# Sums of the lower weights in DRAM at fixed places of each upper block, one quarter to a block and two in the tenth

## The chip, the cores and the metric

The kernel runs on one core of one Trainium2 chip. The metric is the device time of one execution in microseconds (us). Before the change it is 2028.64 us, the median of three runs (2025.68 to 2032.72).

## What is computed

One layer of a streaming encoder on 512 tokens of width 2048, in fp32: a modulated RMS norm, a combined projection into a recurrent and an attention group, an output projection, and then a SwiGLU feed-forward layer of hidden width 5632. Only the last part and its modulation matter here:

```python
mod = c_act @ w_ada[l] + b_ada[l]
sh1, sc1, gt1, sh2, sc2, gt2 = jnp.split(mod, 6, axis=-1)
...
h2 = modulate(rms_norm(x, g_ffn[l]), sh2, sc2)
gate, up = jnp.split(h2 @ w_up[l], 2, axis=-1)
x = x + gt2[:, None, :] * ((jax.nn.silu(gate) * up) @ w_down[l])
```

## The kernel before

Every matrix is split into a high and a low part (`wsplit`: ScalarE rounds the high part in a line at 271, VectorE subtracts it in the line behind, both 128x1024), and each product is three matmuls of 128x512.

The **upper** stage (`h2 @ w_up`) has a short beginning in the ordinary way and then ten blocks, `b` = 0 to 9, of seven products each (`ORDER`: 4, 5, 1, 7, 6, 2, 3), the seven of a Strassen scheme instead of eight. A block needs four units of weights, each two tiles of 128x2048 (`uw`), loaded by SyncE in the order A, C, B, D. In the numbered names `uw3_20` is block 3, unit 2 (0 is A, 1 C, 2 B, 3 D), half 0. VectorE adds one unit into another between products (`sum_unit`). A product has eight steps `j`, each of twelve matmuls for the two steps of one weight split; a half of a product is four steps, so a block has 14 halves. The results of a block are turned in the next one (`back`) and written to DRAM by SyncE (`td`, eight writes a block).

In the upper blocks VectorE also works off the modulation `gt2` in pieces (class `Gt2`): SyncE loads a broadcast row of `c_d` and rows of `adaT` into six pages from step (3, 3) of a block, and VectorE reduces a piece at fixed steps from (4, 1) on.

The **lower** stage (`@ w_down`) follows in four phases. It too is a scheme of seven products over four blocks of `w_down` for each of eleven groups of 512 rows; such a group is called a quarter here, `q` = 0 to 10. Two of its operands, `s2d[q]` and `s4d[q]`, are sums of weights that lie in DRAM. `sums24(q, n)` makes them in four steps: step 0 lets SyncE copy `wdn[0]` into `s2d` and `wdn[1]` into `s4d`, DRAM to DRAM, in halves of 512 KB; steps 1 and 2 let GpSimd add `wdn[2]` and `wdn[3]` into `s2d` with accumulating DMAs; step 3 adds `s2d` into `s4d`. They are first read in phases 2 and 3.

```python
elif n < 3:
    dram_sum(s2d[q], wdn[n + 1, q])
else:
    dram_sum(s4d[q], s2d[q])
```

A scheduler orders each engine's instructions by the order of the code and by priorities (`tc.high_priority`: weight loads, splits and unit sums run `AHEAD` of their place; `tc.issue_after` places an instruction behind another in its queue). Each queue then runs in order: an instruction that waits holds all behind it. The steps of the sums run at the code's own place, and nothing but the data before them holds them at run time.

Before the change a counter over all halves sets the places: from half 2 on, every third half makes the next step, so a quarter takes 12 halves while a block has 14, and a quarter's places wander through the blocks.

Of the kernel before, what the change touches and what calls it, by code (L numbers as in the profile page):

```python
# [60 lines left out]
KEEP = (2, 8, 2)  # L61
GT2_STEPS = ((4, 1), (4, 2), (4, 3), (4, 5), (4, 7), (5, 5), (6, 1))
GT2_N = (6, 6, 6, 6, 6, 6, 7, 7, 7, 7)
SUMS_AT, SUMS_PER = 2, 12
BU_PART = (0, 5, 10, 16)
BUP_STEP = 3
NQ = FT // 4
# [7 lines left out]
def block_kernel(ctx, tc, xT, crow, adaT, vecs, bfr, w1, wyr, wqkv0, wqkv, wgate, wout, wup0, wups, wdn, outT):  # L75
# [17 lines left out]
    def page(name, tag, shape=None):  # L93
        return pgp.tile(shape or [P, S], F32, tag=tag, name=name, bufs=TAGS[tag])
# [180 lines left out]
    def mm(ps, l, r, start, stop):  # L275
        nc.tensor.matmul(ps, lhsT=R(l), rhs=R(r), start=start, stop=stop)  # L276
# [228 lines left out]
    def add(hooks, n, *fns):  # L505
        hooks.setdefault(n, []).extend(fns)
        return hooks
# [587 lines left out]
    def dram_sum(out, src):  # L1095
        for i in range(2):
            cs = slice(i * 1024, (i + 1) * 1024)
            nc.gpsimd.dma_start(out=out[:, cs], in_=src[:, cs], accum_op=ALU.add)  # L1098

    def sums24(q, n):  # L1100
        if n == 0:
            with tc.issue_after((up_loads or stream_loads)[-1]):
                for i in range(2):
                    cs = slice(i * 1024, (i + 1) * 1024)
                    nc.sync.dma_start(out=s2d[q][:, cs], in_=wdn[0, q, :, cs])
                    nc.sync.dma_start(out=s4d[q][:, cs], in_=wdn[1, q, :, cs])
# [4 lines that stand above are left out]
# [36 lines left out]
    NBLK = (FT - 2 * STD) // 4  # L1147
# [24 lines left out]
    def prod_weights(p, b, un):  # L1172
        with tc.high_priority(offset=AHEAD):
            if p == 4:
                un[U_A] = load_unit(b, U_A)
                un[U_C] = load_unit(b, U_C)
            elif p == 5:
                sum_unit(un[U_A], un[U_C])
            elif p == 1:
                un[U_B] = load_unit(b, U_B)  # L1180
            elif p == 7:
                sum_unit(un[U_C], un[U_B])
            elif p == 6:
                sum_unit(un[U_A], un[U_B])
            elif p == 2:
                un[U_D] = load_unit(b, U_D)
            else:
                sum_unit(un[U_A], un[U_D])
            src = un[{4: U_A, 5: U_A, 1: U_B, 7: U_C, 6: U_A, 2: U_D, 3: U_A}[p]]
        for q in range(4):  # L1190
            with tc.high_priority(offset=AHEAD):
                hi, lo = wsplit(src[q // 2][:, (q % 2) * 1024:(q % 2 + 1) * 1024], 1024, f"up{b}_{p}_{q}")
            for i in range(2):
                yield 2 * q + i, hi[:, i * S:(i + 1) * S], lo[:, i * S:(i + 1) * S]

    def back(g, b, f, last=False):
        pt = misc(f"up_t{b}_{f}") if last and f else rgp(f"up_t{b}_{f}")
        for t in range(NT):
            nc.tensor.transpose(out=pt[:, t * P:(t + 1) * P], in_=g[t][:, f * P:(f + 1) * P], identity=ident)
        o = page(f"uo{b}_{f}", "d")  # L1200
        with tc.high_priority(offset=EVAC):
            nc.scalar.activation(o, pt, AF.Copy)
        keep_act(o, 2 * STD + 4 * b + f, last)

    gt2_left = [(r, i) for r in range(4) for i in range(KT)]
    hk = {}
    nprod = halves = 0
    for b in range(NBLK):
        un, keep_ = {}, {}
        gt2 = Gt2(gt2_left[:GT2_N[b]])  # L1210
        del gt2_left[:GT2_N[b]]
        add(hk, (3, 3), gt2.loads)
        for _, at in zip(range(GT2_N[b]), GT2_STEPS):
            add(hk, at, gt2.piece)
        for i, p in enumerate(ORDER):
            pool = misc if (nprod + 2) % 3 == 2 else acc
            nprod += 1
            ps = [pool(f"up{b}_{p}p{t}") for t in range(2)]
            for j, hi, lo in prod_weights(p, b, un):
                th, tl = T[p][j]  # L1220
                for t in range(2):
                    c_ = slice(t * P, (t + 1) * P)
                    mm(ps[t], th[:, c_], hi, j == 0, False)
                    mm(ps[t], th[:, c_], lo, False, False)
                    mm(ps[t], tl[:, c_], hi, False, j == 7)
                for fn in hk.get((i, j), ()):
                    fn()
                if j % 4 == 3:
                    n = halves - SUMS_AT
                    halves += 1  # L1230
                    if 0 <= n < SUMS_PER * NQ and n % SUMS_PER % 3 == 0 and n % SUMS_PER < 12:
                        sums24(n // SUMS_PER, n % SUMS_PER // 3)
            if b + i == 0:
                up_last()
            if p in (4, 5, 1, 7):
                keep_[p] = []
                for t in range(2):
                    w = page(f"us{b}_{p}{t}", "c") if p != 7 else ap_.tile([P, S], F32, tag="x", name=f"us{b}_{p}{t}", bufs=2)
                    with tc.high_priority(offset=EVAC):
                        nc.scalar.activation(w, ps[t], AF.Copy)  # L1240
                    keep_[p].append(w)
            elif p == 6:
                u2 = [page(f"uu{b}_{t}", "c") for t in range(2)]
                s4, s5, s1, s7 = (keep_[k] for k in (4, 5, 1, 7))
                with tc.high_priority(offset=EVAC):
                    for t in range(2):
                        nc.vector.tensor_add(u2[t], ps[t], s1[t])
                with tc.high_priority(offset=POST):
                    for t in range(2):
                        nc.vector.tensor_sub(s7[t], u2[t], s7[t])  # L1250
                        nc.vector.tensor_sub(u2[t], u2[t], s5[t])
                        nc.vector.tensor_sub(s4[t], s4[t], s7[t])
                        nc.vector.tensor_sub(s5[t], s5[t], s7[t])
            else:
                g, u = (s1, s4) if p == 2 else (u2, s5)
                with tc.high_priority(offset=EVAC):
                    for t in range(2):
                        nc.vector.tensor_add(g[t], ps[t], g[t])
                with tc.high_priority(offset=EVAC):
                    for t in range(2):  # L1260
                        nc.scalar.activation(g[t], g[t], AF.Silu)
                        nc.vector.tensor_mul(g[t], g[t], u[t])
        hk = {(1, 1 + 2 * f): [lambda g=s1 + u2, b=b, f=f: back(g, b, f)] for f in range(4)}
# [231 lines left out]
```

## Time and profile before

| | |
|---|---|
| median of three runs | 2028.64 us |
| the profiled execution's own time | 2028.19 us |
| its span, from first to last instruction | 2026.5 us |
| its granted TensorE clock | 0.999 |
| TensorE busy | 2005.5 us (99%), 9330 matmuls |
| VectorE busy | 1678.2 us (83%) |
| ScalarE busy | 986.8 us (49%) |
| GpSimd busy | 109.8 us (5%) |
| DMA queue q1 (SyncE's and ScalarE's issues) | 454.99 MB, 65.4% of 16 engines' span |
| DMA queue q0 (GpSimd's issues) | 39.59 MB, 11.2% |

Rows of the profile name an engine (PE is TensorE, PEld its weight load, DVE VectorE, ACT ScalarE, POOL GpSimd, SP SyncE, with a q for issuing), a line, an operation and output<-input, with buffer numbers left out (`gt` is `gt2_0_12`, `uw` any weight tile). A row of the timeline begins with its start and duration in us and ends with the idle time before it and what ended that. DMA rows give count, KB each and the median us from issue to landing.

### The profile page before, as it was taken

Reading aid. Unit: us, or ns where it says so; the run is one execution under the profiler, and the core shown is the slowest. Engines: PE = TensorE matmul, PEld = TensorE weight load, DVE = VectorE, ACT = ScalarE, POOL = GpSimd, SP = SyncE. Lnnn points to the kernel's source line nnn. Section 1 sums busy time; section 2 is a strip of 40 time slices with the busy share of each in tenths; the row PEclk is TensorE's granted clock in tenths of the full one; section 3 lists DMA queues with packets and bytes.
Section 4 is the critical chain, followed back from the end, with each engine's and each line's share of the span. In section 5 each row is a group of like instructions: output and inputs, shape, how many; then the busy total and the mean of one; then the engine's idle time right before and its main releaser. Section 6 shows DMA issues by size and latency. Waiting matters only on the chain.

```text
span 2026.5 us, 25606 instructions
## 1 busy us (share of the span) xinstructions
PE 2005.5 (99%) x9330; PEld 1688.7 (83%) x9330; DVE 1678.2 (83%) x2300; ACT 986.8 (49%) x1362; POOL 109.8 (5%) x138
## 2 busy tenths in 40 slices
PE   9999999999999999999999999999999999999999
PEld 7889988898888888888887888888888888888887
DVE  8999788877787769898797888988988977777786
ACT  4433446775422257544544544445445455445443
POOL 0000100111000000000010000000000100000000
PEclk9999999999999999999999999999999999999999
DMA  9989866557679874779698868878696677778793
GB/s 354 346 296 336 281 213 209 199 170 258 225 256 319 327 259 143 184 201 270 187 280 236 207 235 228 208 261 238 187 289 186 222 249 245 253 239 295 257 331 119
DMA packets 173683, 496.33 MB, mean 245 GB/s; under 512 B 18434, under 2 KB 41138, under 8 KB 169459
## 3 DMA queue, kind: packets, MB, share of 16 engines
q1 hardware_dynamic: 162372, 454.99, 65.4%
q0 software_dynamic: 11040, 39.59, 11.2%
q8 instruction: 73, 1.20, 0.2%
q14 instruction: 54, 0.44, 0.1%
q10 hardware_dynamic: 144, 0.11, 0.0%
HBM read 458.93 MB, written 93.36 MB: 273 GB/s over the span
## 4 chain that ended last, share of the span: by engine, by line
PE 87%; DVE 6%; issue 4%; DMA 2%; ACT 1%; POOL 0%; DVEq 0%; POOLq 0%; ACTq 0%
PE up_2p L276 5%; PE up_6p L276 5%; PE up_3p L276 5%; PE up_5p L276 5%; PE up_1p L276 5%; PE up_7p L276 5%; PE up_4p L276 5%; PE w1p L276 4%; PE dn4p L276 3%; PE dn6p L276 3%; PE dn3p L276 3%; PE dn1p L276 3%; PE dn2p L276 3%; PE dn7p L276 3%; PE dn5p L276 3%
## 5 line engine op out<-in xcount | busy, mean ns | idle before, releaser
L1170 DVE TENSOR_TENSOR uw<-uw,uw 128x2048 f32<-128x2048 f32 x80 | 182.5, 2282 | 2.0 <-DMA uw<-in_wups 2.0
L178 DVE SCALAR_TENSOR_TENSOR ada<-ada,c_b 128x1024 f32<-128x1024 f32 x96 | 116.7, 1221 | 46.3 <-DMA ada<-in_adaT 46.1
L271 ACT ACTIVATE up_1h<-uw 128x1024 fp32r<-128x1024 f32 x70 | 74.4, 1063 | 118.9 <-PE up_6p L276 21.6
L271 ACT ACTIVATE up_0h<-uw 128x1024 fp32r<-128x1024 f32 x70 | 74.3, 1062 | 115.0 <-PE up_4p L276 16.6
L272 DVE TENSOR_TENSOR up_1l<-uw,up_1h 128x1024 fp32r<-128x1024 f32 x70 | 85.3, 1219 | 36.1 <-ACT up_1h L271 36.1
L272 DVE TENSOR_TENSOR up_0l<-uw,up_0h 128x1024 fp32r<-128x1024 f32 x70 | 85.4, 1220 | 33.6 <-ACT up_0h L271 33.5
L271 ACT ACTIVATE up_3h<-uw 128x1024 fp32r<-128x1024 f32 x70 | 74.4, 1063 | 71.7 <-PE up_2p L276 14.9
L271 ACT ACTIVATE up_2h<-uw 128x1024 fp32r<-128x1024 f32 x70 | 74.2, 1060 | 58.4 <-PE up_2p L276 16.5
L272 DVE TENSOR_TENSOR up_2l<-uw,up_2h 128x1024 fp32r<-128x1024 f32 x70 | 85.3, 1218 | 20.0 <-ACT up_2h L271 19.9
L272 DVE TENSOR_TENSOR up_3l<-uw,up_3h 128x1024 fp32r<-128x1024 f32 x70 | 85.2, 1217 | 10.3 <-ACT up_3h L271 10.3
L1098 POOL DMA_DIRECT2D s2d<-in_wdn x44 | 36.5, 842 | 624.2 <-DMA s2d<-in_wdn 624.2
L276 PE MATMUL w1p<-hph,w1l 128*128 128x512 f32 x128 | 49.8, 389 | 0.0
L276 PE MATMUL w1p<-hpl,w1h 128*128 128x512 f32 x128 | 49.8, 389 | 0.0
L222 DVE SCALAR_TENSOR_TENSOR gt<-gt,gt_None 128x512 f32<-128x512 f32 x64 | 43.0, 683 | 5.5 <-DMA gt<-in_adaT 5.5
L276 PE MATMUL w1p<-hph,w1h 128*128 128x512 f32 x128 | 42.6, 392 | 0.0
L188 DVE SCALAR_TENSOR_TENSOR ada<-ada,c_b 128x1024 f32<-128x1024 f32 x32 | 39.0, 1218 | 4.0 <-DMA ada<-in_adaT 4.0
L188 DVE SCALAR_TENSOR_TENSOR adf<-adf,c_b 128x1024 f32<-128x1024 f32 x32 | 39.0, 1219 | 0.3 <-DMA adf<-in_adaT 0.3
L631 ACT ACTIVATE bt<-bt,nm 128x128 f32<-128x128 f32 (+3 forms) x32 | 17.9, 561 | 34.8 <-DVE nm L629 34.5
L712 DVE SCALAR_TENSOR_TENSOR ba<-bw,sh,ba 128x512 f32<-128x512 f32 x45 | 32.2, 743 | 0.0
L616 POOL TENSOR_SCALAR_AFFINE_SELECT bt<-bt 128x128 f32<-128x128 f32 x32 | 22.8, 735 | 116.2 <-ACT bt L615 116.2
L437 ACT ACTIVATE hph<-x,A 128x512 fp32r<-128x512 f32 x16 | 11.6, 723 | 35.0 <-DVE A L434 35.0
L276 PEld LDWEIGHTS w1p<-hph,w1h 128*128 128x128 f32 x128 | 24.0, 188 | 5.4 <-issue 0.6
(2293 smaller groups left out, 6637.8 us busy)
## 6 DMA issues: line engine op xcount, KB each, us to landing
uw<-in_wups SPq DMA_DIRECT2D x160, 512.0 KB, 7.2
ada<-in_adaT SPq DMA_DIRECT2D x128, 512.0 KB, 5.4
s2d<-in_wdn POOLq DMA_DIRECT2D x44, 512.0 KB, 8.8
adf<-in_adaT SPq DMA_DIRECT2D x32, 512.0 KB, 6.0
gt<-in_adaT SPq DMA_DIRECT2D x64, 256.0 KB, 6.1
s2d<-in_wdn SPq DMA_DIRECT2D x22, 512.0 KB, 8.9
s4d<-in_wdn SPq DMA_DIRECT2D x22, 512.0 KB, 9.9
s4d<-s2d POOLq DMA_DIRECT2D x22, 512.0 KB, 8.2
```

What stands on the lines that cost most here:

```text
L178: nc.vector.scalar_tensor_tensor(out=t, in0=t, scalar=1.0, in1=cs, op0=ALU.mult, op1=ALU.mult, accum_out=ac)
L188: nc.vector.scalar_tensor_tensor(out=t, in0=t, scalar=1.0, in1=c_b[:, cs], op0=ALU.mult, op1=ALU.mult, accum_out=ada_acc[j][:, hf, i:i + 1])
L222: nc.vector.scalar_tensor_tensor(out=t, in0=t, scalar=1.0, in1=c, op0=ALU.mult, op1=ALU.mult, accum_out=gt2_acc[:, r, i:i + 1])
L271: tail_hi.append(nc.scalar.activation(R(hi[:, :n]), raw_ap, AF.Copy).ins)
L272: tail_lo.append(nc.vector.tensor_sub(R(lo[:, :n]), raw_ap, hi[:, :n]).ins)
L276: nc.tensor.matmul(ps, lhsT=R(l), rhs=R(r), start=start, stop=stop)
L437: nc.scalar.activation(R(h), xt, AF.Copy, scale=a)
L616: nc.gpsimd.affine_select(out=bt[:, b * P:n], in_=bt[:, b * P:n], pattern=[[-1, P]], compare_op=ALU.is_ge, fill=NEG, base=0, channel_multi ...
L631: nc.scalar.activation(p[:, :n], p[:, :n], AF.Exp, scale=-1.0, bias=nm, accum_out=sm)
L712: nc.vector.scalar_tensor_tensor(out=ba[j], in0=src, scalar=s1, in1=ba[j], op0=ALU.mult, op1=ALU.add)
L1098: nc.gpsimd.dma_start(out=out[:, cs], in_=src[:, cs], accum_op=ALU.add)
L1170: nc.vector.tensor_add(d_, d_, s_)
```

## The change

The counter goes. In blocks 0 to 8 the four steps of quarter `b` are made behind halves 1, 3, 9 and 12 of the block; in block 9 those of quarters 9 and 10 behind halves 0, 2, 4, 6 and 7, 9, 11, 13.

```diff
-SUMS_AT, SUMS_PER = 2, 12
+SUMS_STEPS = {1: 0, 3: 1, 9: 2, 12: 3}
+SUMS_LAST = {0: (9, 0), 2: (9, 1), 4: (9, 2), 6: (9, 3), 7: (10, 0), 9: (10, 1), 11: (10, 2), 13: (10, 3)}
...
-    nprod = halves = 0
+    nprod = 0
...
                 if j % 4 == 3:
-                    n = halves - SUMS_AT
-                    halves += 1
-                    if 0 <= n < SUMS_PER * NQ and n % SUMS_PER % 3 == 0 and n % SUMS_PER < 12:
-                        sums24(n // SUMS_PER, n % SUMS_PER // 3)
+                    n = 2 * i + j // 4
+                    if b < NBLK - 1 and n in SUMS_STEPS:
+                        sums24(b, SUMS_STEPS[n])
+                    elif b == NBLK - 1 and n in SUMS_LAST:
+                        sums24(*SUMS_LAST[n])
```

Weights are loaded ahead, so the rows around block 3's C and B units on SyncE's queue (`uw3_1` and `uw3_2`) run during block 2. Before, with `s2d3` and `s4d3` of quarter 3 and `s2d4`, `s4d4` of quarter 4, up to the first `td` write of block 3:

```order
L1105 DMA s2d3_6899<-in_wdn 128x1024
L1106 DMA s4d3_6910<-in_wdn 128x1024
L1105 DMA s2d3_6899<-in_wdn 128x1024
L1106 DMA s4d3_6910<-in_wdn 128x1024
L1163 DMA uw3_10_9505<-in_wups 128x1024 x2
L1163 DMA uw3_11_9508<-in_wups 128x1024 x2
L1163 DMA uw3_20_9702<-in_wups 128x1024 x2
L1163 DMA uw3_21_9705<-in_wups 128x1024 x2
L1105 DMA s2d4_6900<-in_wdn 128x1024
L1106 DMA s4d4_6911<-in_wdn 128x1024
L1105 DMA s2d4_6900<-in_wdn 128x1024
L1106 DMA s4d4_6911<-in_wdn 128x1024
```

The same place after the change:

```order
L1164 DMA uw3_10_9499<-in_wups 128x1024 x2
L1164 DMA uw3_11_9502<-in_wups 128x1024 x2
L1106 DMA s2d3_6899<-in_wdn 128x1024
L1107 DMA s4d3_6910<-in_wdn 128x1024
L1164 DMA uw3_20_9700<-in_wups 128x1024 x2
L1106 DMA s2d3_6899<-in_wdn 128x1024
L1164 DMA uw3_21_9703<-in_wups 128x1024 x2
L1107 DMA s4d3_6910<-in_wdn 128x1024
```

Quarter 4's four copies left this place for the one block later, and quarter 3's moved from ahead of C to around B. Before, quarter 8's copies stood on SyncE's queue between block 7's units in this same way:

```order
L1163 DMA uw7_10_11958<-in_wups 128x1024 x2
L1163 DMA uw7_11_11961<-in_wups 128x1024 x2
L1105 DMA s2d8_6904<-in_wdn 128x1024
L1106 DMA s4d8_6915<-in_wdn 128x1024
L1163 DMA uw7_20_12159<-in_wups 128x1024 x2
L1105 DMA s2d8_6904<-in_wdn 128x1024
L1163 DMA uw7_21_12162<-in_wups 128x1024 x2
L1106 DMA s4d8_6915<-in_wdn 128x1024
```

These rows of before are what the change makes of every block from 2 to 9. The tenth block has more. Around its C and B units on SyncE's queue, which run during block 8, stood, before, quarter 10's copies alone, ahead of C; after the change the rows from C on are:

```order
L1164 DMA uw9_10_13178<-in_wups 128x1024 x2
L1164 DMA uw9_11_13181<-in_wups 128x1024 x2
L1106 DMA s2d9_6905<-in_wdn 128x1024
L1107 DMA s4d9_6916<-in_wdn 128x1024
L1164 DMA uw9_20_13379<-in_wups 128x1024 x2
L1106 DMA s2d9_6905<-in_wdn 128x1024
L1164 DMA uw9_21_13382<-in_wups 128x1024 x2
L1107 DMA s4d9_6916<-in_wdn 128x1024
L1106 DMA s2d10_6906<-in_wdn 128x1024
L1107 DMA s4d10_6917<-in_wdn 128x1024
L1106 DMA s2d10_6906<-in_wdn 128x1024
L1107 DMA s4d10_6917<-in_wdn 128x1024
```

Eight copies stand there instead of four. On GpSimd's queue the end of the sums was, before, with the first late `td` write behind it:

```order
L1098 DMA s2d9_6905<-in_wdn 128x1024 x4
L1098 DMA s4d9_6916<-s2d9_6905 128x1024 x2
L1098 DMA s2d10_6906<-in_wdn 128x1024 x4
L1098 DMA s4d10_6917<-s2d10_6906 128x1024 x2
L1088 DMA td3_10_6895<-uo9_1_13860 256x1x256
```

After the change the same twelve sums stand there, with two of quarter 9's and one of quarter 10's exchanged:

```order
L1099 DMA s2d9_6905<-in_wdn 128x1024 x3
L1099 DMA s4d9_6916<-s2d9_6905 128x1024
L1099 DMA s2d9_6905<-in_wdn 128x1024
L1099 DMA s2d10_6906<-in_wdn 128x1024
L1099 DMA s4d9_6916<-s2d9_6905 128x1024
L1099 DMA s2d10_6906<-in_wdn 128x1024 x3
L1099 DMA s4d10_6917<-s2d10_6906 128x1024 x2
L1089 DMA td3_10_6895<-uo9_1_13860 256x1x256
```

Before, quarter 9's copies stood a block earlier than quarter 10's; now both stand in front of the tenth block, and so do their sums.

## Prediction

> **What bounds the kernel now.** I read the page first, then TensorE's waits, then the busy time of each upper block, then the queues around the one block that stands out. Blocks are counted from 0, as `b` in the code; "the tenth" is block 9. Times "in a block" run from its first matmul.
>
> ```profile
> span 2026.5 us, 25606 instructions
> PE 2005.5 (99%) x9330; PEld 1688.7 (83%) x9330; DVE 1678.2 (83%) x2300; ACT 986.8 (49%) x1362; POOL 109.8 (5%) x138
> ...
> PE up_6p L276 <- DVE up_2l L272: 3.6, 1, 3.6
> PE up_6p L276 <- DVE up_1l L272: 1.3, 1, 1.3
> ```
>
> TensorE is busy for 99% of the span. The two last rows are its waits between 800 and 1600 us, where all ten upper blocks lie: two waits, both in product 6, both on a VectorE split. The next rows give stretches cut at the first matmuls of blocks 2, 3, 4, 6, 7 and 9 (span, then busy time and count of PE, PEld, DVE, ACT and POOL, granted clock, DMA share, GB/s), and last the 4 us of the longer wait.
>
> ```profile
> 968.00:1046.40 78.40, 78.31 (x353) 64.58 (x352) 67.97 (x77) 38.23 (x44) 4.10 (x5) 1.00 0.75 225
> 1046.40:1131.70 85.30, 80.42 (x354) 65.57 (x353) 67.73 (x75) 38.19 (x44) 6.57 (x8) 0.98 0.86 236
> 1131.70:1209.80 78.10, 78.10 (x353) 64.56 (x352) 67.43 (x75) 38.21 (x44) 4.94 (x6) 1.00 0.80 217
> ...
> 1366.10:1444.20 78.10, 78.10 (x353) 64.56 (x352) 68.12 (x78) 38.21 (x44) 8.22 (x10) 1.00 0.93 256
> 1522.40:1600.60 78.20, 78.20 (x354) 64.61 (x353) 68.83 (x79) 39.26 (x46) 0.81 (x1) 1.00 0.63 202
> 1102.00:1106.00 4.00, 3.06 (x10) 2.45 (x11) 4.00 (x7) 0.00 (x0) 0.00 (x0) 0.79 0.78 311
> ```
>
> A block takes 78.1 to 78.2 us with TensorE busy throughout. Block 3 takes 85.3: 7.1 too many, of which 85.30 - 80.42 = 4.9 are waiting and 2.2 slower matmuls, at a granted clock of 0.79 behind the longer wait. Block 2 has 0.2 too many. So all that the upper stage can give back is 7.3 us, 0.36% of the time.
>
> Where block 3 loses it: VectorE's rows there, then the same ones in block 9.
>
> ```profile
> 1087.75 1.23 DVE L272 TENSOR_TENSOR up_0l<-uw,up_0h 128x1024 fp32r<-128x1024 f32 x1 [1.49 <-ACT up_0h L271]
> 1094.43 0.69 DVE L222 SCALAR_TENSOR_TENSOR gt<-gt,gt_None 128x512 f32<-128x512 f32 x1 [5.46 <-DMA gt<-in_adaT]
> ...
> 1099.46 2.29 DVE L1170 TENSOR_TENSOR uw<-uw,uw 128x2048 f32<-128x2048 f32 x1 [1.96 <-DMA uw<-in_wups]
> 1101.67 1.22 DVE L272 TENSOR_TENSOR up_2l<-uw,up_2h 128x1024 fp32r<-128x1024 f32 x1
> ...
> 1564.91 0.68 DVE L222 SCALAR_TENSOR_TENSOR gt<-gt,gt_None 128x512 f32<-128x512 f32 x1
> 1571.06 1.22 DVE L272 TENSOR_TENSOR up_2l<-uw,up_2h 128x1024 fp32r<-128x1024 f32 x1
> ```
>
> VectorE takes its work in order. In block 3 it stands 5.46 us before the first gt2 piece, whose load is late, then 1.96 before the sum into unit A, for the D weights; the split that TensorE needs is behind both. It starts at 1101.67, 55.3 us into the block; in block 9 at 48.7.
>
> Why the loads are late: GpSimd's sums in DRAM still run then. First the twelve sums of quarters 3 and 4 in blocks 2 and 3 (first, seventh and last), then the six of quarter 8 in blocks 6 and 7.
>
> ```profile
> 1025.26 0.84 POOL L1098 DMA_DIRECT2D s2d<-in_wdn  x1 [54.36 <-DMA s2d<-in_wdn]
> ...
> 1059.47 0.81 POOL L1098 DMA_DIRECT2D s2d<-in_wdn  x1 [7.17 <-DMA s2d<-in_wdn]
> ...
> 1082.23 0.81 POOL L1098 DMA_DIRECT2D s4d<-s2d  x1 [4.67 <-DMA s2d<-in_wdn]
> ...
> 1357.99 0.82 POOL L1098 DMA_DIRECT2D s2d<-in_wdn  x1 [46.97 <-DMA s2d<-in_wdn]
> 1368.57 1.65 POOL L1098 DMA_DIRECT2D s2d<-in_wdn  x2 [9.77 <-DMA s2d<-in_wdn]
> 1376.89 0.81 POOL L1098 DMA_DIRECT2D s4d<-s2d  x1 [6.67 <-DMA s2d<-in_wdn]
> 1379.37 0.84 POOL L1098 DMA_DIRECT2D s2d<-in_wdn  x1 [1.67 <-DMA s2d<-in_wdn]
> 1388.27 0.82 POOL L1098 DMA_DIRECT2D s4d<-s2d  x1 [8.05 <-DMA s2d<-in_wdn]
> ```
>
> Each sum waits for the one before it on the same half. With a landing of 8.2 us (the page's row for s4d, last of the next fence), quarter 8's end at 1396.5, 30 us into block 7. Quarter 4's, stuck behind quarter 3's, end at 1092.7, 46 us into block 3: the last two took 10.5 us to land. The next rows are SyncE's issue of the gt2 loads and of the D and A weights in block 3; the landing of the gt2 loads and of quarter 4's last sums there, and of the gt2 loads in block 7; of the weights issued from 1086 in block 3 and from 1556 in block 9; and the page's two rows for the sums.
>
> ```profile
> 1077.52 8.35 SPq L211 DMA_DIRECT2D gt<-in_adaT  x5
> 1086.00 11.21 SPq L1163 DMA_DIRECT2D uw<-in_wups  x8
> ...
> gt<-in_adaT SPq DMA_DIRECT2D x5, 256.0 KB, 13.2
> s4d<-s2d POOLq DMA_DIRECT2D x2, 512.0 KB, 10.5
> ...
> gt<-in_adaT SPq DMA_DIRECT2D x5, 256.0 KB, 4.8
> ...
> uw<-in_wups SPq DMA_DIRECT2D x3, 512.0 KB, 12.1
> ...
> uw<-in_wups SPq DMA_DIRECT2D x3, 512.0 KB, 5.5
> ...
> s2d<-in_wdn POOLq DMA_DIRECT2D x44, 512.0 KB, 8.8
> ...
> s4d<-s2d POOLq DMA_DIRECT2D x22, 512.0 KB, 8.2
> ```
>
> The gt2 loads are issued some 30 us into a block. Where sums are still in flight they take 13.2 us instead of 4.8, and D takes 12.1 instead of 5.5.
>
> **The change, part by part.** No instruction is added or removed: 44 copies and 66 sums stay, of the same sizes. TensorE, VectorE and ScalarE have the same order as before; only SyncE's and GpSimd's queues are moved.
>
> *Blocks 2 to 8: minus 7.3 us.* Quarter 4's copies no longer follow quarter 3's in one block. Each quarter has its copies around the B weights and its six sums after that, the layout that quarter 8 has now. Block 7, which follows it, takes 78.1 us; so I take 78.1 for each: minus 7.1 in block 3, minus 0.2 in block 2. Bounds: nothing to gain if block 3's stall had another cause, and 7.3. I take 7.3, because the quarter 8 row is this very layout. What the moved copies pass on SyncE is the C weights (now ahead of the copies) and half of B (now behind three copies); TensorE has no wait in block 7, where B stands so too, and this price is nothing. If B's slack were gone the next thing late would be product 1's split.
>
> *The tenth: plus 9.5 us.* Two quarters share block 9. SyncE issues eight copies just before it, around the B weights; GpSimd then has twelve sums in a row, as in blocks 2 and 3. No wait ties them to TensorE's progress, so the later steps of the list do not hold them back. The first sum starts where quarter 8's does, 1357.99 against block 7's start at 1366.1, so 8 us before the block. When the twelfth lands decides. In blocks 2 and 3 twelve sums took from 1025.26 to 1092.7, 5.6 us each; quarter 8's last five took 1368.57 to 1396.5, 5.6 each as well. With two quarters to interleave GpSimd can fill gaps (1379.37 to 1388.27 is one), so the other bound is two sums in every 8.8, 4.4 each. Twelve by 4.4 to 5.6 from 8 us ahead end 45 to 59 us into block 9. I take 52, the middle: gaps are there to be filled, but four extra copies stand beside the first sums.
>
> So gt2's loads and D's of block 9 meet the sums as in block 3, where they ended at 46. The row it is nearest to is block 3's, 7.1 us. The gt2 loads there had sums beside them nearly all the time, so they land no later; D's would land later by part of the 6 us that the sums last longer. I put 0.4 of it on the path, between none and all: 7.1 + 2.4 = 9.5. Bounds: zero (loads of 4.8 us; the split has slack, as block 9's row above shows) and 7.1 + (59 - 46) = 20.1. A gain is excluded, since block 9 has no wait now. Queued behind the two stalled VectorE rows are the gt2 pieces, the sum into A and the splits of product 6, and TensorE waits for these.
>
> *Behind block 9.* The last `td` writes and the first reads of the sums:
>
> ```profile
> 1608.15 0.75 POOL L1088 DMA_DIRECT2D td<-uo  x1 [82.92 <-ACT uo L1202]
> ...
> L1276 SPq DMA_DIRECT2D dq_1r<-s2d x2: 327/355/383, 1804.4 to 1804.8; - x2
> ```
>
> GpSimd's queue is needed next at 1608, 27 us after the latest end of the sums, 1522.4 + 59 = 1581, and the sums are read from 1804. Price nothing; it would cost only if the sums ran past 1608.
>
> Sum, against the profiled execution's 2028.19 us (span 2026.5; the median of the runs is 0.45 higher): 2028.2 - 7.3 + 9.5 = 2030.4, so 2030.
>
> One rule of the Trainium skill speaks for another end: "DMA: Bandwidth & Descriptors", section "Anatomy of one DMA — SWDGE (gpsimd) path", fits a DMA that GpSimd issues as about 2.0 us plus its bytes at 436 GB/s, an estimate of 3.2 us for 512 KB. By it the twelve sums would be over before the gt2 loads and the time 2021. The page's row for these accumulating transfers has 8.8 us, so the sum goes by that.
>
> **The rivals.** *The stall is gone altogether.* If two quarters interleave so well that D's and gt2's loads come clear, block 9 takes 78.2 and the time is 2028.2 - 7.3 = 2020.9; 2022 with a rest of 1. For it: block 9 now has the lowest DMA share of the rows above, 0.63. Against it: 45 us is the earliest end by rows, and the gt2 loads go at 30. The page's rule above would end here too, by its own 3.2 us.
>
> *Slower.* D's loads fall in the sums' time as a whole. Past 14 us in block 9 (2034.9) the kernel is slower by over 0.3%: with block 3's 7.1 that is where D lands 7 us later than there. With 16 the time is 2037, at the bound of 20.1 it is 2041. For it: eight copies instead of four ahead of the sums. Against it: D is issued in the same place and queue 1 keeps moving beside sums.
>
> *The change does not do what it says* can be left out for blocks 2 to 9, as the order shows it done; quarters 0 and 1 stay where they were.
>
> **How the numbers follow.** My forecast, a stall that moves from block 3 to block 9 with 2 to 14 us there (2022.9 to 2034.9): 0.58. The stall gone, below 2022.5: 0.22. Over 14 us: 0.20. The bound of 0.3%, about what a measurement of this kernel can tell from no change, is 6.1 us, so these three are same, faster and slower. The range is 2020.5 to 2037: from the stall gone to 16 us in block 9; what lies between 16 and 20.1 is the part left out.
>
> **What would show it.** In the changed kernel: block 3 of 78.1 us without a wait; block 9 of some 88, with TensorE's two waits on the splits of product 6 there, VectorE waiting for gt2 in front of them, and gt2's landing near 13 us; twelve sums up to 50 us into block 9. Wrong it would be if block 9 took 78.2, or if any of blocks 4 to 8, which get quarter 8's layout, took over 79.

## The result and the profile after

The changed kernel takes 2039.74 us (median of 4 runs, 2038.21 to 2040.86); the kernel before took 2028.47 beside it (4 runs). The ratio is 1.0051, 95% interval 1.0038 to 1.0064: slower by half a percent, above the range of the prediction. The profiled execution took 2038.21 us. Its page begins (compare the first fence of the prediction):

```profile
span 2036.5 us, 25603 instructions
...
PE 2007.5 (99%) x9330; PEld 1689.8 (83%) x9330; DVE 1679.3 (82%) x2300; ACT 986.9 (48%) x1362; POOL 110.4 (5%) x138
```

The span is 10.0 us longer. TensorE's waits between 800 and 1620 us are again two, both on splits of product 6:

```profile
PE up_6p L277 <- DVE up_1l L273: 5.5, 1, 5.5
PE up_6p L277 <- DVE up_2l L273: 5.2, 1, 5.2
```

Blocks 3 and 9, cut at the first matmul of each (columns as in the prediction: span, busy time and count of PE, PEld, DVE, ACT, POOL, granted clock, DMA share, GB/s):

```profile
1047.69:1125.82 78.13, 78.13 (x353) 64.57 (x352) 67.46 (x75) 38.22 (x44) 4.96 (x6) 1.00 0.81 223
1516.52:1610.60 94.08, 83.39 (x354) 67.69 (x353) 69.14 (x79) 39.23 (x46) 9.11 (x11) 0.93 0.91 242
```

Block 3 is whole: 78.13 instead of 85.3. Block 9 has 94.08 instead of 78.2, 15.9 too many: 94.08 - 83.39 = 10.7 of waiting, and 83.39 - 78.2 = 5.2 of slower matmuls, at a mean granted clock of 0.93 over the block. This execution also has 1.3 us more ahead of block 0, and with them the spans agree: 1.3 - 7.1 + 15.9 = 10.1. Blocks 4 to 8 take 78.1 to 78.2. Block 2 keeps its extra 0.3 (78.45).

VectorE in block 9, the rows that answer to those of block 3 before (what is in brackets is its idle time ahead of the row, and for whom):

```profile
1557.90 1.23 DVE L273 TENSOR_TENSOR up_0l<-uw,up_0h 128x1024 fp32r<-128x1024 f32 x1 [1.49 <-ACT up_0h L272]
1568.76 0.69 DVE L223 SCALAR_TENSOR_TENSOR gt<-gt,gt_None 128x512 f32<-128x512 f32 x1 [9.64 <-DMA gt<-in_adaT]
...
1577.76 2.29 DVE L1171 TENSOR_TENSOR uw<-uw,uw 128x2048 f32<-128x2048 f32 x1 [5.94 <-DMA uw<-in_wups]
1579.97 1.22 DVE L273 TENSOR_TENSOR up_2l<-uw,up_2h 128x1024 fp32r<-128x1024 f32 x1
```

It is the picture of block 3 with larger numbers: 9.64 us for gt2 where 5.46 stood, 5.94 for D where 1.96 stood. The split that ends TensorE's second wait (the last row) starts 63.5 us into the block; it was 55.3 in block 3 and 48.7 in the undisturbed block 9. GpSimd's first sums and its last:

```profile
1507.43 0.81 POOL L1099 DMA_DIRECT2D s2d<-in_wdn  x1 [48.41 <-DMA s2d<-in_wdn]
1517.78 1.68 POOL L1099 DMA_DIRECT2D s2d<-in_wdn  x2 [9.54 <-DMA s2d<-in_wdn]
...
1566.56 0.81 POOL L1099 DMA_DIRECT2D s4d<-s2d  x1 [4.59 <-issue]
```

The first starts 9.1 us ahead of block 9. The second and third, which run beside quarter 10's copies, took 12.4 and 15.4 us to land. The last landed 9.6 us after its issue, 59.6 us into the block. Now SyncE's issues behind that: the queue in block 9, and what it waited for between 1530 and 1570 us (in total, times, longest).

```profile
1550.68 11.60 SPq L212 DMA_DIRECT2D gt<-in_adaT  x5
1562.37 6.65 SPq L1164 DMA_DIRECT2D uw<-in_wups  x4
```

```profile
SPq L212 <- DMA td<-uo: 7.7, 3, 4.9
SPq L1164 <- DMA gt<-in_adaT: 2.9, 1, 2.9
SPq L1164 <- DMA gt_None<-c_d: 2.2, 1, 2.2
```

The five gt2 loads need 11.6 us to be issued. They wait for pages that the `td` writes still read (in the code both come from the same group of buffers). D's loads stand behind them, and two of the four wait once more, until a gt2 load has landed. So D is issued from 45.8 us into the block on, against 34.5 in the block 9 of before. Landing times in the two block 9, after (1530 to 1570 us) and then before (1535 to 1575 us; median us in the last column):

```profile
uw<-in_wups SPq DMA_DIRECT2D x4, 512.0 KB, 13.7
gt<-in_adaT SPq DMA_DIRECT2D x5, 256.0 KB, 11.1
td<-uo SPq DMA_DIRECT2D x4, 256.0 KB, 13.9
td<-tu SPq DMA_DIRECT2D x2, 256.0 KB, 16.6
td<-tw SPq DMA_DIRECT2D x2, 128.0 KB, 13.0
```

```profile
uw<-in_wups SPq DMA_DIRECT2D x4, 512.0 KB, 5.5
gt<-in_adaT SPq DMA_DIRECT2D x7, 256.0 KB, 6.3
td<-uo SPq DMA_DIRECT2D x4, 256.0 KB, 2.4
...
td<-tu SPq DMA_DIRECT2D x2, 256.0 KB, 2.5
...
td<-tw SPq DMA_DIRECT2D x2, 128.0 KB, 1.9
```

Beside the sums everything on SyncE's queue is slower, the `td` writes most of all: 13.0 to 16.6 us instead of 1.9 to 2.5.

### The profile page after: what moved, and what is told of

It reads as the page before. It is cut to its first block, busy times and chain, and to the rows that moved or that the text cites. A ratio compares the mean times of both kernels' runs of the same rounds, so it can differ in the third digit from the quotient of the medians.

```text
span 2036.5 us, 25603 instructions
## 1 busy us (share of the span) xinstructions
PE 2007.5 (99%) x9330; PEld 1689.8 (83%) x9330; DVE 1679.3 (82%) x2300; ACT 986.9 (48%) x1362; POOL 110.4 (5%) x138
## 3 DMA queue, kind: packets, MB, share of 16 engines
q0 software_dynamic: 11040, 39.59, 11.6%
## 4 chain that ended last, share of the span: by engine, by line
PE 86%; issue 7%; DVE 3%; DMA 3%; POOL 1%; ACT 0%; SPq 0%; DVEq 0%; POOLq 0%; ACTq 0%
PE up_5p L277 5%; PE up_1p L277 5%; PE up_7p L277 5%; PE up_2p L277 5%; PE up_3p L277 5%; PE up_6p L277 5%; PE up_4p L277 5%; PE w1p L277 4%; PE dn3p L277 3%; PE dn4p L277 3%; PE dn6p L277 3%; PE dn2p L277 3%; PE dn1p L277 3%; PE dn7p L277 3%; PE dn5p L277 3%
## 5 line engine op out<-in xcount | busy, mean ns | idle before, releaser
L179 DVE SCALAR_TENSOR_TENSOR ada<-ada,c_b 128x1024 f32<-128x1024 f32 x96 | 116.8, 1223 | 45.3 <-DMA ada<-in_adaT 45.2
L272 ACT ACTIVATE up_0h<-uw 128x1024 fp32r<-128x1024 f32 x70 | 74.3, 1062 | 122.5 <-PE up_4p L277 16.6
L272 ACT ACTIVATE up_2h<-uw 128x1024 fp32r<-128x1024 f32 x70 | 74.2, 1060 | 57.9 <-PE up_6p L277 16.6
L273 DVE TENSOR_TENSOR up_3l<-uw,up_3h 128x1024 fp32r<-128x1024 f32 x70 | 85.3, 1219 | 10.3 <-ACT up_3h L272 10.3
L632 ACT ACTIVATE bt<-bt,nm 128x128 f32<-128x128 f32 (+3 forms) x32 | 18.0, 561 | 39.9 <-DVE nm L630 39.6
L438 ACT ACTIVATE hph<-x,A 128x512 fp32r<-128x512 f32 x16 | 11.6, 725 | 34.8 <-DVE A L435 34.7
```

The costliest lines, as they stand in the source:

```text
L179: nc.vector.scalar_tensor_tensor(out=t, in0=t, scalar=1.0, in1=cs, op0=ALU.mult, op1=ALU.mult, accum_out=ac)
L272: tail_hi.append(nc.scalar.activation(R(hi[:, :n]), raw_ap, AF.Copy).ins)
L273: tail_lo.append(nc.vector.tensor_sub(R(lo[:, :n]), raw_ap, hi[:, :n]).ins)
L438: nc.scalar.activation(R(h), xt, AF.Copy, scale=a)
L632: nc.scalar.activation(p[:, :n], p[:, :n], AF.Exp, scale=-1.0, bias=nm, accum_out=sm)
```

## The experiments

All start from the changed kernel. "Too many" is what a block takes over the 78.2 us of an undisturbed one.

**Copies without their sums.** Of quarter 10 only the first step, the four copies, is left; its sums are left out:

```
-SUMS_LAST = {0: (9, 0), 2: (9, 1), 4: (9, 2), 6: (9, 3), 7: (10, 0), 9: (10, 1), 11: (10, 2), 13: (10, 3)}
+SUMS_LAST = {0: (9, 0), 2: (9, 1), 4: (9, 2), 6: (9, 3), 7: (10, 0)}
```

> The changed kernel without the six sums of quarter 10 (its four copies stay; s2d and s4d of quarter 10 then hold unsummed weights). Theory 'sums': the 16 us that block 9 takes too long come from GpSimd's accumulating sums, which run beside the loads until 59 us into the block; without quarter 10's they end near 30, block 9 takes 78 to 80 us and the time is 2021 to 2025. Rival 'copies': the eight copies piled ahead of the block fill queue 1 and make the td writes and all behind them late; block 9 stays at 88 us or more and the time at 2033 or more.

Measured: 2024.21 us in its one run, span 2022.5, block 9 at 78.2, and no wait of TensorE in the upper stage. Quarter 9's six sums ended 33.8 us into the block. So eight copies alone cost nothing; it takes the second six sums.

**Twelve sums without quarter 10's copies beside them.** These copies go to block 4, and block 9's second six sums are added to quarter 9's tensors, so the output leaves quarter 10's sums out:

```
-... 7: (10, 0), 9: (10, 1), 11: (10, 2), 13: (10, 3)}
+... 9: (9, 1), 11: (9, 2), 13: (9, 3)}
...
+                    if (b, n) == (4, 8):
+                        sums24(10, 0)
```

> The reverse: quarter 10's four copies are made in block 4 and its six sums are replaced by six of the same size on quarter 9's tensors (so twelve sums, four copies ahead of block 9; quarter 9's sums are counted twice and quarter 10's left out). Theory 'sums': block 9 takes 90 us or more, time 2035 to 2041. Rival 'copies': block 9 takes 78 to 82 us, time 2021 to 2026. The eight copies now stand ahead of block 4 with six sums: 'sums' expects 78 to 79 us for it, 'copies' a stall there of 8 us or more.

Measured: 2029.15 us in its one run, span 2027.4, block 9 at 84.7, 6.5 too many, with one wait instead of two:

```profile
PE up_6p L277 <- DVE up_2l L273: 3.6, 1, 3.6
```

This lies between the two expectations. Twelve sums and gt2's loads are enough for a stall, but the four copies in front make it more than twice as long. Block 4, with eight copies and six sums, took 78.16. One thing is mixed here: the twelve sums hang in one chain on the same tensors. The last two experiments part that.

**The double in another block.** Quarters 4 and 5 share block 4, all other blocks have one quarter:

```
-                    if b < NBLK - 1 and n in SUMS_STEPS:
-                        sums24(b, SUMS_STEPS[n])
-                    elif b == NBLK - 1 and n in SUMS_LAST:
-                        sums24(*SUMS_LAST[n])
+                    if b != 4 and n in SUMS_STEPS:
+                        sums24(b + (b > 4), SUMS_STEPS[n])
+                    elif b == 4 and n in SUMS_LAST:
+                        q, step = SUMS_LAST[n]
+                        sums24(q - 5, step)
```

> The two quarters share block 4 (quarters 4 and 5) instead of block 9; blocks 5 to 9 have quarters 6 to 10, one each. Theory 'sums': the stall goes with them: block 4 takes 90 us or more, block 9 78.2, time 2035 to 2041. Rival 'place': the tenth block's stall is larger than block 3's was because of what only it has (seven gt2 pieces, the first loads of the lower stage behind): block 4 takes 83 to 87 us, about as block 3 before, and the time is 2026 to 2031.

Measured: 2036.9 us (5 runs), ratio to before 1.0033 (1.0020 to 1.0045). Block 9 is back at 78.2, and block 4 takes 92.57, 14.4 too many:

```profile
PE up_6p L277 <- DVE up_2l L273: 10.6, 1, 10.6
PE up_6p L277 <- DVE up_1l L273: 1.6, 1, 1.6
```

The stall goes with the double quarter; that the tenth block is the last has little to do with it.

**Quarter 10 behind D.** Its copies are called behind D's loads and its last sums at the start of the lower stage:

```
+SUMS_LAST = {1: (9, 0), 3: (9, 1), 9: (9, 2), 12: (9, 3), 11: (10, 0), 13: (10, 1)}
...
+            if ph == 0 and n == 1 and q in (0, 1):
+                sums24(10, 2 + q)
```

> Quarter 10's copies are made only behind block 9's D weights and the first loads of the lower stage, its sums then run beside the end of block 9 and the first phase below; one quarter per block up to 9. Theory 'sums': block 9 takes 78 to 79 us. If the first phase below has slack for six sums the time is 2020 to 2024, faster than before by 0.2 to 0.4%. Rival 'given back': the first phase's loads are as sensitive as gt2's; it loses 5 us or more and the time is 2027 to 2034.

Measured: 2030.25 us (12 runs), ratio to before 0.9998 (0.9987 to 1.0009). Blocks 1 to 9 take 78.1 to 78.2 but for the 0.3 of block 2, and block 0 its 76.2 as before: the 7.1 us are won there. They are lost in the first product of the lower stage. The next rows are TensorE's wait, that stretch and VectorE's longest wait in it, then two kinds of the loads issued between 1580 and 1605 us (weights, and `td` read back as the product's other operand), and last the same stretch of the kernel before.

```profile
PE up_t L1200 <- DVE uu L1264: 4.7, 1, 4.7
```

```profile
1593.40:1612.70 19.30, 14.46 (x65) 11.76 (x64) 12.29 (x17) 8.77 (x13) 3.92 (x6) 0.91 0.78 239
```

```profile
1601.13 0.69 DVE L1309 TENSOR_TENSOR dq_1tl<-dq_1tl,dq_1th 128x512 fp32r<-128x512 f32 x1 [6.66 <-ACT dq_1th L1307]
```

```profile
dq_3r<-in_wdn SPq DMA_DIRECT2D x2, 512.0 KB, 16.6
...
dq_1tl<-td SPq DMA_DIRECT2D x2, 256.0 KB, 16.9
```

```profile
1600.60:1613.20 12.60, 12.60 (x65) 10.62 (x64) 12.41 (x17) 8.38 (x12) 3.39 (x5) 1.00 0.28 87
```

The low DMA share of 0.28 there was not spare. The sums met the lower stage's first loads, which took 17 us; VectorE stood 6.66 us before the split of one of them, and the row that TensorE waits for comes behind that split. The product took 19.3 us instead of 12.6. The gain was given back.

**No gt2 work in block 9.** Its seven loads and pieces go to the other blocks; the double stays.

```
-GT2_STEPS = (..., (5, 5), (6, 1))
-GT2_N = (6, 6, 6, 6, 6, 6, 7, 7, 7, 7)
+GT2_STEPS = (..., (5, 5), (6, 1), (6, 3))
+GT2_N = (7, 7, 7, 7, 7, 7, 7, 7, 8, 0)
```

> The changed kernel with block 9 relieved of its seven gt2 loads and pieces: they are done one more in each block before (7 in blocks 0 to 7, 8 in block 8). The two quarters stay together in block 9, with all copies and all twelve sums. Theory (the queue): block 9 is long because the gt2 loads wait on SyncE for pages that slow td writes still hold, and D's loads stand behind them in that queue and VectorE's work behind the gt2 pieces. Without them D is issued some 34.5 us into the block instead of 45.8; with the 15 us that D took to land it is there at 50, about when its split is due: block 9 takes 82 us or less (4 too many at most, of 15.9), the time is 2022 to 2026. Rival (bandwidth alone): D is late because the sums keep the DMA engines until 59.6 us into the block, whenever it is issued: block 9 takes 88 or more and the time is 2032 or more. Between 82 and 88 each has a half. Should one of blocks 0 to 8 become longer than 79 us, the seventh gt2 piece was not free there.

Measured: 2031.82 us (10 runs), ratio to before 1.0016 (1.0004 to 1.0027). Blocks 0 to 8 are as in the changed kernel, block 9 takes 85.6, 7.4 too many: between the two expectations again. TensorE's wait, VectorE's row ahead of it, and the DMA queues while D's loads were in flight (1553 to 1578 us; packets, MB, share of 16 engines; then the landing of D's):

```profile
PE up_6p L277 <- DVE up_2l L273: 5.7, 1, 5.7
```

```profile
1572.17 2.29 DVE L1171 TENSOR_TENSOR uw<-uw,uw 128x2048 f32<-128x2048 f32 x1 [8.22 <-DMA uw<-in_wups]
```

```profile
q0 software_dynamic: 724, 2.61, 59.6%
q1 hardware_dynamic: 1933, 4.23, 45.3%
...
uw<-in_wups SPq DMA_DIRECT2D x4, 512.0 KB, 18.0
```

Taking gt2's work out of block 9 is worth 15.9 - 7.4 = 8.5 us. D was issued at 34.5, as expected, but it took 18 us and not the expected 15: VectorE could add its first half at 53.5 (the row above), and its last landing is at 58.4. The packets of the sums took 60% of the 16 engines' time in these 25 us. The edit takes away two things at once, the loads that stand ahead of D on SyncE's queue and the DMA time of those loads, and this run alone does not part them.

**Neither quarter 10's copies nor gt2 loads.** The second and the fifth edit together:

> Both halves taken away at once: quarter 10's four copies in block 4 (and the second six sums of block 9 added to quarter 9's tensors instead of quarter 10's, so the output leaves quarter 10's sums out and has quarter 9's twice), and no gt2 loads in block 9 (7 in blocks 0 to 7, 8 in block 8). What is left of the double is twelve sums beside D's loads. With the copies away block 9 had 6.5 too many, with the gt2 loads away 7.4, with neither 15.9. Theory (the two delay D by separate ways, the copies through the end of the sums, the gt2 loads through SyncE's queue): D is issued at 35 us and the sums end at some 50 to 54, so D lands by 50 and block 9 has 2 us too many or less, time 2021 to 2027 by where the run starts. Rival (D is slowed by the sums alone, and each of the two took away only part of the same time): 4 us too many or more.

Measured: 2023.09 us in its one run, span 2021.4, block 9 at 78.2, no wait. The queues in the same stretch of time, and D's landing over it:

```profile
q1 hardware_dynamic: 1977, 6.00, 63.0%
q0 software_dynamic: 423, 1.53, 30.7%
...
uw<-in_wups SPq DMA_DIRECT2D x2, 512.0 KB, 7.9
```

Twelve sums alone, with D issued at 34.5, cost nothing; D's last landing is at 48.2. The theory's number held, 2 us too many or less. The one chain of sums is part of this kernel too, and it too leaves quarter 10's sums out.

**No block has two quarters.** Quarter 0 goes to the second of the ordinary groups ahead of block 0, and block b gets quarter b+1:

```
+        if gi == 1:
+            for n in range(4):
+                add(hk, 1 + 3 * n, lambda n=n: sums24(0, n))
...
+                    if n in SUMS_STEPS:
+                        sums24(b + 1, SUMS_STEPS[n])
```

> No block has two quarters: quarter 0's copies and sums are called in the second of the ordinary groups ahead of block 0, and block b has quarter b+1, at the fixed steps of the changed kernel. Theory (only the double does harm): no block has a TensorE wait, every block takes 78.1 to 78.5 us (block 0: 76.2), and nothing is given back in the lower stage, since block 9's six sums end 30 to 40 us into it: 2028.2 less the 7.3 of blocks 2 and 3, so 2020 to 2023, faster than before by 0.25 to 0.4%. Rival (no free place): the group ahead of block 0 or block 0 itself, where weights for both kinds of group are loaded, loses 4 us or more to the four copies and six sums there: 2024 to 2030, and the loss is seen ahead of block 1.

Measured: 2025.19 us (12 runs) beside 2029.38 for the kernel before (23 runs), ratio 0.9984 (0.9971 to 0.9997). The profiled span is 2020.7, 5.8 less than before. Blocks 3 and 9 of it, and its one wait in the upper stage:

```profile
1047.70:1125.80 78.10, 78.10 (x353) 64.58 (x352) 67.43 (x75) 38.21 (x44) 4.96 (x6) 1.00 0.79 224
1516.60:1594.70 78.10, 78.10 (x353) 64.55 (x352) 68.72 (x79) 39.24 (x46) 4.10 (x5) 1.00 0.78 228
```

```profile
PE up_4p L276 <- DVE up_3l L272: 0.3, 1, 0.3
```

No block stalls. Block 0 takes 77.2 instead of 76.16, so 1 us is lost there, far from the rival's 4. In its profiled execution the gain is 7.1 - 1.0 = 6.1 in the blocks. The runs show less of it: their median is above the 2020 to 2023 that were expected, and their gain of 0.16% (0.6 to 5.9 us by the interval) is short of the expected 0.25 to 0.4%. Of the kernels here that do all the sums and were run several times, it is the one that is faster than both.

**Only the copies moved.** Quarter 10's copies go to block 4, its six sums stay in block 9 on their own tensors:

```
+            with tc.issue_after(last_sum[9, 1]) if q == 10 else nullcontext():
...
+                    if (b, n) == (4, 8):
+                        sums24(10, 0)
```

> The changed kernel with one edit: quarter 10's four copies are issued in block 4. Its six sums stay in block 9, on its own tensors, held behind quarter 9's first sums on GpSimd; all twelve sums are done as in the changed kernel. It parts two things that the run without quarter 10's sums of its own had mixed: there the copies were early, and the twelve sums hung in one chain on quarter 9's tensors, so that 1.5 of them were in flight on average between 30 and 45 us of the block, where the changed kernel has 2.4. Theory (in flight): with two quarters two chains run side by side, GpSimd's queue takes the larger share of the DMA engines, and D's loads and the td writes get less; the copies matter little: 2.2 or more in flight at 30 to 45 us and block 9 10 us or more too long (88 or more). Rival (copies): the four copies ahead of B only push the sums back by 6 us, which is what D meets: block 9 as in the run with one chain, 84 to 86.

Measured: 2026.54 us in its one run, span 2024.8, block 9 at 84.2, 6.0 too many: the rival's number. The waits, the block, the first sum and the last:

```profile
PE up_6p L277 <- DVE up_2l L273: 3.6, 1, 3.6
PE up_6p L277 <- DVE up_1l L273: 0.2, 1, 0.2
```

```profile
1514.70:1598.90 84.20, 80.39 (x353) 65.57 (x352) 69.05 (x79) 39.24 (x46) 9.06 (x11) 0.98 0.91 247
```

```profile
1507.36 0.81 POOL L1102 DMA_DIRECT2D s2d<-in_wdn  x1 [48.24 <-DMA s2d<-in_wdn]
...
1550.32 0.81 POOL L1102 DMA_DIRECT2D s4d<-s2d  x1 [5.86 <-DMA s2d<-in_wdn]
```

With 9.7 us of landing the last ends 45.3 us into the block: twelve sums in 52.7 us, 4.4 each. In the changed kernel they need 68.7 us, 5.7 each. They went side by side, 2.9 in flight on average between 15 and 30 us of the block, and only 1.7 were left between 30 and 45 us, where the theory had 2.2 or more. The rival's reason was too small: without the copies the sums end 14.3 us earlier, not 6. Moving the four copies is worth 15.9 - 6.0 = 9.9 us.

**One quarter after the other.** The copies stay, quarter 10's sums are held behind quarter 9's last:

```
+            with tc.issue_after(last_sum[9, 3]) if q == 10 else nullcontext():
```

> The changed kernel with one edit: quarter 10's six sums are held behind quarter 9's last on GpSimd's queue, so that the two quarters go one after the other; all copies stay where the change puts them. Theory (in flight): at most two sums are in flight, D's loads and the td writes keep the larger share, gt2 and D come earlier though the sums end no earlier (58 to 64 us): block 9 has 8 us too many or less (86 or less), time 2023 to 2031. Rival (end of the sums): what counts is how long the sums last into the block: 14 us too many or more, 2036 or more. If its sums ran on to 70 us and D were still on time, the number in flight would be shown; if both are late it is not told apart.

Measured: 2038.99 us (4 runs), ratio to before 1.0054 (1.0037 to 1.0071), block 9 at 94.1, 15.9 too many:

```profile
PE up_6p L277 <- DVE up_2l L273: 12.5, 1, 12.5
PE up_6p L277 <- DVE up_1l L273: 1.2, 1, 1.2
```

The sums end at 62.7 us. The rival held. The edit did not lower the number in flight where it was meant to (2.2 between 30 and 45 us, 2.4 in the changed kernel), so it says little on the number in flight; it does show that another order on GpSimd's queue, with the copies where they are, wins nothing.

**All of them together.** For each block, from the issues and landings of its loads and sums: the time that sums were in flight between 30 and 60 us of the block, added over the sums; the first recorded landing of gt2's loads and the last recorded one of D's, in us of the block; and where VectorE starts the sum into unit A, which needs D's first half and ahead of which it waits if that is late.

| kernel, block | sums in flight, us | first gt2 | D, last | sum into A | too many |
|---|---|---|---|---|---|
| before, 3 | 26 | 47.9 | 56.8 | 53.0 | 7.1 |
| changed, 9 | 57 | 53.0 | 62.3 | 61.2 | 15.9 |
| copies without sums, 9 | 4 | 39.8 | 46.3 | 46.5 | 0 |
| sums in one chain, copies early, 9 | 31 | 45.9 | 54.2 | 51.5 | 6.5 |
| double in block 4, 4 | 57 | 48.3 | 62.9 | 60.5 | 14.4 |
| one after the other, 9 | 61 | 51.0 | 62.9 | 61.9 | 15.9 |
| only the copies moved, 9 | 25 | 47.5 | 53.1 | 52.0 | 6.0 |
| no double, 9 | 0 | 37.2 | 44.5 | 46.5 | 0 |
| no gt2 loads, 9 | 59 | none | 58.4 | 53.5 | 7.4 |
| neither copies nor gt2 loads, 9 | 33 | none | 48.2 | 45.7 | 0 |

Where gt2's loads are in the block, the loss is about a quarter of the sums' time behind 30 us. What ends the stall is one row in all seven blocks that lose time: VectorE's sum into unit A, which waits for D's first half and has the last splits of product 6 behind it. Undisturbed it starts 46.5 us into the block; each block loses its delay and 0.4 to 1.5 us more (the changed kernel 61.2 - 46.5 = 14.7, for 15.9 lost). Moving the copies won 9.9 us and moving gt2's work 8.5, together more than the 15.9 there were: each brings this one row forward, by 9.2 and 7.7 us, and ahead of 46.5 us there is nothing left to win.

The splits that TensorE waits for need neither gt2 nor D. In the code product 6 reads unit A before D is added to it, and in the changed kernel ScalarE had rounded the last high part of product 6 by 49.5 us into block 9, while the split behind the sum started at 63.5. They are late only because VectorE takes its rows in order and the gt2 piece and the sum stand ahead of them. D itself is first needed in product 2, the next one. No run here moves the sum behind the splits, so what that would win is open.

## Why the prediction was wrong

**What held.** The minus of block 3 was 7.1 as its row said; only the 0.2 of block 2, counted with it, has another cause and stayed. Blocks 4 to 8 kept 78.1. The stall moved to block 9, to the same two splits of product 6, with gt2 and D in front of them. Nothing changed behind block 9.

**The step that failed** is the size of one term, "The tenth: plus 9.5 us". It measured 15.9. The prediction had made it up of 7.1 + 0.4 × 6, and both factors of the second part were too small.

- *The sums' end.* The prediction took 52 us, the middle between 45 and 59, because "gaps are there to be filled". They ended at 59.6. The two bounds were two real cases: without the copies beside them the sums end at 45.3 (4.4 each), with the copies at 59.6 (5.7 each). The change has the copies there, so the upper bound was the value to take. With the 0.4 kept, it gives 7.1 + 0.4 × 13.6 = 12.5: 3.0 of the missing 6.4 us. Two ends in the rows of before were also misread, because a median landing stood in for the last one: quarter 4's last sum took 11.9 us and ended 47.7 us into block 3, not 46, and quarter 8's took 5.6 and ended 27.8 us into block 7, so its last five went at 5.1 each and not 5.6. With 47.7 the 3.0 becomes 2.4.
- *The share on the path.* 15.9 is 7.1 + 0.65 × 13.6, so the share was 0.65 and not 0.4: the other 3.4 us (4.0 with 47.7, at a share of 0.74). The prediction held that gt2's loads "land no later" than in block 3. VectorE got the first of them 52.2 us into the block instead of 48.0. The slow writes of `td` kept the pages for which these loads wait, and D's loads, next on the same queue, were issued from 45.8 on instead of 39.6. VectorE could add D's first half at 61.2 instead of 53.0: 6.2 of these 8.2 us are the later issue, 2.0 a longer landing. Without gt2's loads 8.5 of the 15.9 are gone.

**The rival "slower"**, from 14 us on in block 9, is what came, and by the reason that was named for it, eight copies instead of four ahead of the sums. Its own condition was D 7 us later than in block 3; it was 8.2. The reason against it, that D is issued in the same place, is true of the order and false of the time. The rest of the miss is not the change: the sum with 15.9 is 2028.2 - 7.1 + 15.9 = 2037.0, and this profiled execution had 1.3 us more ahead of block 0. The other three runs took 1.0 to 2.7 us longer than it and have no trace.

**The rule weighed there**, from the Trainium skill, "DMA: Bandwidth & Descriptors", section "Anatomy of one DMA — SWDGE (gpsimd) path", gives an estimate of 3.2 us for a DMA of 512 KB that GpSimd issues. These runs disagree for accumulating ones, and the measurement decides: the quickest sum in any of the kernels above took 5.3 us from issue to landing, half of the changed kernel's 66 took 8.0 or more, and its last twelve went at 5.7 us each, with 2.4 in flight on average between 30 and 45 us of the block.

## What to carry to other kernels

A background stream of DMAs is priced by what is in flight when the critical loads are issued, and by what stands in front of it. When a rate has two bounds, ask which condition makes each, and take the one whose condition the change sets up; here the copies set the slow one. And follow a slow transfer through the buffers it holds to the queue that waits for them: with gt2's loads waiting for such buffers ahead of D the price was 15.9 us, without them 7.4, and moving the last quarter later only moved the collision to the next stage's first loads. Last, ask whether the row that the critical engine waits for is itself late, or only stands in order behind one that is: here the splits were ready.

## What was not expected of the hardware

- Writes of `td`, 128 and 256 KB, suffered most beside the sums: 2.4 us became 13.9, 2.5 became 16.6 and 1.9 became 13.0, a factor of 6 to 7, while D's loads of 512 KB went from 5.5 to 13.7, a factor of 2.5.
- A third of the stall is not waiting: 5.2 of the 15.9 us are slower matmuls, and the granted clock was down to 0.50 in 4 us behind each wait (1570 to 1574 and 1582 to 1586 us). This does not make the block longer by as much. With one quarter after the other the same 15.9 us are 13.7 of waiting and 2.2 of slower matmuls: those between the two waits fill time in which TensorE would have waited for D anyway. In the kernel without gt2 loads, with one wait of 5.7 us, 1.7 us are slower matmuls.
- Sums of 512 KB took 12 to 15 us beside four plain copies in DRAM (block 9's second and third sum in the changed kernel), and 6 to 8 us in the same place without them (only the copies moved).
- The packets of the sums' queue take about twice the time for a byte: in the 25 us shown above for the kernel without gt2 loads, 59.6% of the 16 engines' time for 2.61 MB (23% for a MB) against 45.3% for 4.23 MB (11%) on the other queue. (The two shares add up to more than 100%, so packets of the two queues overlap in time.)
